# Latent heads of block 1: where 1 / z is multiplied in a two-block transformer kernel

## The chip, the core and the metric
The kernel runs on one core of one Trainium2 chip. The metric is the time of one execution in device microseconds (us): 780.84 us is the median of three runs of the kernel before, 778.87 us and 781.52 us are the lowest and the highest. A smaller time is better. Engines are called as the profile calls them: PE (matrix products), DVE, ACT and POOL (element-wise work), SP (issues the DMAs).

## The reference, cut to what matters
Two transformer blocks are computed for 256 latent tokens of width 1024, with 256 context tokens in the first block. The change lies in the first block's second group of heads, the latent heads (`B_HEADS = 8`), whose queries and keys come out of low-rank projections:

```python
def _softmax_attend(q, k, v):
    scale = (B_NOPE + B_ROPE) ** -0.5
    s = jnp.einsum('bqhd,bkhd->bhqk', q, k).astype(jnp.float32) * scale
    a = jax.nn.softmax(s, axis=-1)
    return jnp.einsum('bhqk,bkhe->bqhe', a.astype(v.dtype), v)
```

q has 256 rows and k and v 512 (context and latent tokens together), a head's q and k are 96 wide, v is 64 wide. The softmax is exp(s - max) divided by its sum z along a row. The outputs of these heads and of the four differential heads (`_diff_attend`) are joined and multiplied by `w_out`; then come a gated feed-forward layer, a norm, and the second block.

## The kernel before
Activations are kept with channels on the 128 partitions and tokens along the free axis. A weight matrix is streamed in pieces of 1 MB into `raw` buffers (three of them), and every half of a piece is split into a rounded part `hi` (ACT copies) and a rest `lo` (DVE subtracts); a linear layer issues three products for each 128x128 block (`lin`, `wout_part`).

All instructions are recorded first and put in order by a planner (`Rec.schedule`, from line 485): a list scheduler with costs of its own for every instruction (`cost`, from line 439), which starts at each step the instruction that can start earliest, and breaks ties by the order of the program. It knows that two-input instructions of DVE and those of POOL can hold each other up ("port" in `cost`). For the tags in `STRICT` (`raw`, `hi`, `lo`, `la`, `tp`, `mm`, `s`, `v5` among them) buffers are given out in the order of the program. Every engine then runs its own list in order. Since all instructions are emitted by one line (666), the profile's groups are told apart by their tiles: `s` and `v` (for `v5`) are score banks, `tp` is a pair of banks for transposes and small sums, `la` is the single bank of an attention output, `mm` holds linear layers, `c` is any tile of 256 or 512 columns, `col` one of a few columns.

The stage of the latent heads runs over four pairs (`for hp in range(4)`, line 1328). `unit(softB2, pvB2, hp)` records the softmax of both heads of a pair, and then the output of the pair before it (`flush`). `softB` does, for each of two tiles of 128 queries (`qt`): scores 128x512 into a bank, a row maximum (DVE), its scaling (DVE), the exponential with the row sum z (ACT), the reciprocal of z (DVE), and a multiplication of the 128x512 probabilities by it: on POOL for `qt` 0, on DVE for `qt` 1 (`POOL_B = (0,)`). `pvB2` transposes the probabilities of both heads with the identity into `tp` banks, four 128x128 transposes to a bank (`transposed`, line 1162), copies each bank out on ACT, multiplies by `vB` into `la`, head 0 of the pair on the output rows 0 to 63 and head 1 on rows 64 to 127, and splits the result into the `hi` and `lo` halves of a tile of `cat`.

Beside these heads run the end of the differential heads, `gemv` (line 975: rows of `ada2` in a `raw` buffer times a row vector `crow`; after `h0` the pieces 7, after `h1` 8 and 9, after `h3` 10 and 11; for all of these but 9 the product is POOL's, 128x1024, twice for each piece, and ACT sums it), and the parts of `w_out` on finished tiles of `cat` (`wout_part`: two after pair 1, two after pair 2, two after pair 3, two after the last output). Behind the stage come the other half of `w_out` (banks `s` and `v5`), the residual, and the feed-forward layer.

Of the kernel before, what the change touches and what calls it, by code (L numbers as in the profile page):

```python
# [14 lines left out]
AF = mybir.ActivationFunctionType  # L15
OP = mybir.AluOpType
# [200 lines left out]
POOL_A, POOL_B, POOL_N = (1,), (0,), (0, 1)  # L217
# [461 lines left out]
def _build(ctx, tc, nc, A, out):  # L679
# [7 lines left out]
    V, ACT, G, PE, SP = (rec.eng(e) for e in ("V", "ACT", "G", "PE", "SP"))  # L687

    def own(pool, name, tag, shape, dt):

        def make():
            t = f"{tag}s{v.root.slot}"
            return pool.tile(shape, dt, tag=t, name=name, bufs=1)
        v = rec.root(tag, shape, dt, make)
        return v

    def T(tag, shape, dt=F32):
        cnt[0] += 1
        name = f"{tag}_{cnt[0]}"
        return own(sp, name, tag, shape, dt)  # L700
# [7 lines left out]
    def PS(tag, shape):  # L708
        cnt[0] += 1
        name = f"{tag}_{cnt[0]}"  # L710
        return own(pp, name, tag, shape, F32)

    def mm(o, a, b, start, stop):
        PE.matmul(o, a, b, start=start, stop=stop)

    def mm2(o, a, b, start, stop):
        return PE.matmul(o, a, b, start=start, stop=stop, skip_group_check=True)
# [3 lines left out]
    def PSR(shape, tags):  # L721
        k = rot[tags] = rot.get(tags, -1) + 1
        return PS(tags[k % len(tags)], shape)
# [4 lines left out]
    def c1(dt=F32, n=256):  # L728
        return T("c1", [128, n], dt)

    def c2(dt=F32):
        return T("c2", [128, 512], dt)
# [24 lines left out]
    ident = cst.kid((slice(None), slice(0, 128)))  # L757
# [209 lines left out]
    def split(dst_h, dst_l, src):  # L967
        ACT.activation(dst_h, src, AF.Copy)
        V.tensor_tensor(dst_l, src, dst_h.bitcast(F32), OP.subtract)
# [192 lines left out]
    def transposed(p):  # L1162

        r = []
        for kp in range(2):
            tp = PS("tp", [128, 512])
            for z in range(2):
                kt = 2 * kp + z
                for qt in range(2):
                    o = 256 * z + 128 * qt  # L1170
                    PE.transpose(tp[:, o:o + 128], p[qt][:, 128 * kt:128 * kt + 128], ident)
            t = c2()
            ACT.activation(t, tp, AF.Copy)
            r += [t[:, 0:256], t[:, 256:512]]
        return r

    cat = []
    scA, scB = 64 ** -0.5, 96 ** -0.5
# [40 lines left out]

    def softB(h):  # L1220
        pa = []
        for qt in range(2):
            tq = slice(128 * qt, 128 * qt + 128)
            mx = T("col", [128, 4])
            s_ = PSR([128, 512], SC)
            mm(s_, qB[h][0:96, tq], kB[h][0:96], True, True)
            V.tensor_reduce(mx[:, 0:1], s_, AX.X, OP.max)
            V.tensor_scalar(mx[:, 1:2], mx[:, 0:1], -scB, None, op0=OP.mult)
            p = c2()
            ACT.activation(p, s_, AF.Exp, bias=mx[:, 1:2], scale=scB, accum_out=mx[:, 2:3])  # L1230
            V.reciprocal(mx[:, 3:4], mx[:, 2:3])
            (G if qt in POOL_B else V).tensor_scalar(p, p, mx[:, 3:4], None, op0=OP.mult)
            pa.append(p)
        return pa

    def softB2(hp):
        return softB(2 * hp), softB(2 * hp + 1)

    def pvB2(hp, pas):
        o_ = PS("la", [128, 256])  # L1240
        aT = [transposed(pa) for pa in pas]
        for kt in range(4):
            for z in range(2):
                h = 2 * hp + z
                mm2(o_[64 * z:64 * z + 64], vB[kt][:, 64 * h:64 * h + 64], aT[z][kt], kt == 0, kt == 3)
        c_ = c2(F32R)
        split(c_[:, 0:256], c_[:, 256:512], o_)
        cat.append(c_)

    pend = []  # L1250
# [77 lines left out]
    for hp in range(4):  # L1328
        unit(softB2, pvB2, hp)
        gemvs(f"h{hp}")  # L1330
        for kc in WOUT_AT.get(hp, ()):
            wout_part(kc)
# [21 lines left out]
    for m in range(8):  # L1354
        if m < 4:
            ps = woa[m // 2][:, m % 2]
        else:
# [7 lines left out]
                               op0=OP.mult, op1=OP.subtract)  # L1365
# [154 lines left out]
    for m in range(8):  # L1520
# [6 lines left out]
                               op0=OP.mult, op1=OP.subtract)  # L1527
# [270 lines left out]
    for qt in range(2):  # L1798
# [21 lines left out]
        o_ = PS("la", [128, 512])  # L1820
        gs = [slice(0, 64), slice(64, 128)]
        tp = PS("tp", [128, 128])
# [4 lines left out]
        for j in range(4):  # L1827
            p = [(c2 if qt else c1)().rearrange("p (a b) -> p a b", a=2) for _ in range(2)]
            mx, zs = T("col", [128, 8]), T("col", [128, 2, 2])
# [12 lines left out]
            for br in range(2):  # L1842
                for g in range(2):
                    ACT.activation(p[g][:, br, 0:nk], p[g][:, br, 0:nk], AF.Exp, bias=mx[:, 4 + 2 * br + g:5 + 2 * br + g],
                                   accum_out=zs[:, br, g:g + 1])
# [9 lines left out]
        for kt in range(qt + 1):  # L1855
            for br in range(2):
                n_ += 1
                ts = []
                for g in range(2):
                    tp = PS("tp", [128, 512])  # L1860
# [34 lines left out]
    for m in range(4):  # L1895
# [5 lines left out]
        s_ = c2(F32R)  # L1901
# [6 lines left out]
    for m in range(8):  # L1908
        pb = PSR([128, 256], LIN)
        lin(pb, BASE["proj"] + 8 * m, 4, lambda kc: nsa[kc][:, 0:256], lambda kc: nsa[kc][:, 256:512])  # L1910
        pa = PSR([128, 256], LIN)
        lin(pa, BASE["proj"] + 8 * m + 4, 4, lambda kc: ssm[kc][:, 0:256], lambda kc: ssm[kc][:, 256:512])
        s_ = sg[m]
# [60 lines left out]
```

## Time and profile before

| | us |
|---|---|
| median of three runs | 780.84 |
| lowest and highest run | 778.87, 781.52 |
| the profiled execution, its own time | 778.39 |
| span of the profiled execution, first to last instruction | 776.6 |
| PE busy in the span | 743.9 (96%) |
| DVE busy | 583.5 (75%) |
| ACT busy | 430.8 (55%) |
| POOL busy | 304.9 (39%) |

The span is 1.8 us shorter than that execution's own time. Busy shares are averages over stages with different limits. Matmuls are pipelined and their ends are modelled, so a PE that is shown busy need not be at its peak. The stage of the latent heads lies between about 144 us and 194 us. Groups are read by tile names, for the reason given above. "Idle before" beside an instruction is the time in which its engine had nothing to run, with what ended it.

### The profile page before, as it was taken

Reading aid. Unit: us, or ns where it says so; the run is one execution under the profiler, and the core shown is the slowest. Engines: PE = TensorE matmul, PEld = TensorE weight load, DVE = VectorE, ACT = ScalarE, POOL = GpSimd, SP = SyncE. Lnnn points to the kernel's source line nnn. Section 1 sums busy time; section 2 is a strip of 40 time slices with the busy share of each in tenths; the row PEclk is TensorE's granted clock in tenths of the full one; section 3 lists DMA queues with packets and bytes.
Section 4 is the critical chain, followed back from the end, with each engine's and each line's share of the span. In section 5 each row is a group of like instructions: output and inputs, shape, how many; then the busy total and the mean of one; then the engine's idle time right before and its main releaser. Section 6 shows DMA issues by size and latency. Waiting matters only on the chain.

```text
span 776.6 us, 15213 instructions
## 1 busy us (share of the span) xinstructions
PE 743.9 (96%) x5987; PEld 675.2 (87%) x5987; DVE 583.5 (75%) x1106; ACT 430.8 (55%) x786; POOL 304.9 (39%) x313
## 2 busy tenths in 40 slices
PE   5998999999999999999999997899999999999998
PEld 3877785557999999999999996498899999999997
DVE  6768787977999899888668898976488666654552
ACT  6435439887765365555554432578556666643441
POOL 0013154764041949998012175686250333310000
PEclk9999899999999999999999999999999999999999
DMA  8956633434597366554666621053364655556540
GB/s 332 364 212 229 217 132 114 177 108 176 204 270 273 110 257 230 181 201 167 214 227 214 214 84 55 1 170 157 110 208 173 213 172 212 180 208 199 203 176 14
DMA packets 33993, 142.88 MB, mean 184 GB/s; under 512 B 11777, under 2 KB 15233, under 8 KB 17794
## 3 DMA queue, kind: packets, MB, share of 16 engines
q1 hardware_dynamic: 33922, 141.91, 51.7%
q8 instruction: 47, 0.77, 0.4%
q14 instruction: 24, 0.20, 0.1%
HBM read 139.54 MB, written 1.05 MB: 181 GB/s over the span
## 4 chain that ended last, share of the span: by engine, by line
PE 86%; DVE 8%; ACT 3%; DMA 1%; issue 1%; POOL 0%; SPq 0%; DVEq 0%
PE mm L666 42%; PE s L666 32%; PE tp L666 6%; DVE c L666 5%; PE la L666 4%; PE v L666 3%; ACT c L666 2%; DVE lo L666 1%; DVE col L666 1%; DMA raw<-in_ada 1%; DMA k_X<-in_x 0%; DVE raw L666 0%; DVE k_adc L666 0%; ACT raw L666 0%; ACT hi L666 0%
## 5 line engine op out<-in xcount | busy, mean ns | idle before, releaser
L666 DVE TENSOR_TENSOR lo<-raw,hi 128x1024 fp32r<-128x1024 f32 x206 | 263.0, 1280 | 82.3 <-ACT hi L666 81.0
L666 ACT ACTIVATE hi<-raw 128x1024 fp32r<-128x1024 f32 x206 | 216.2, 1053 | 193.1 <-PE mm L666 94.3
L666 PE MATMUL mm<-xs,hi 128*128 128x256 f32 (+1 forms) x992 | 179.6, 282 | 0.6 <-ACT hi L666 0.4
L666 PEld LDWEIGHTS mm<-xs,hi 128*128 128x128 f32 x992 | 151.4, 188 | 3.2 <-issue 1.4
L666 PE MATMUL mm<-c,hi 128*128 128x256 f32 (+1 forms) x744 | 141.8, 289 | 4.6 <-DVE c L666 2.7
L666 PE MATMUL mm<-xs,lo 128*128 128x256 f32 (+1 forms) x496 | 138.5, 280 | 2.0 <-DVE lo L666 2.0
L666 PEld LDWEIGHTS mm<-c,hi 128*128 128x128 f32 x744 | 115.1, 190 | 14.3 <-issue 4.7
L666 PE MATMUL s<-xs,hi 128*128 128x256 f32 (+1 forms) x672 | 123.0, 283 | 0.0
L666 PE MATMUL s<-c,hi 128*128 128x256 f32 (+1 forms) x676 | 120.2, 278 | 0.0
L666 PE MATMUL mm<-c,lo 128*128 128x256 f32 (+1 forms) x372 | 106.4, 287 | 1.2 <-DVE lo L666 1.2
L666 PEld LDWEIGHTS s<-c,hi 128*128 128x128 f32 x676 | 103.2, 188 | 1.4 <-issue 0.4
L666 PEld LDWEIGHTS s<-xs,hi 128*128 128x128 f32 x672 | 102.9, 188 | 0.7 <-issue 0.4
L666 PEld LDWEIGHTS mm<-xs,lo 128*128 128x128 f32 x496 | 93.8, 189 | 2.8 <-DVE lo L666 2.2
L666 PE MATMUL s<-xs,lo 128*128 128x258 f32 (+1 forms) x336 | 94.1, 280 | 2.2 <-DVE lo L666 2.2
L666 PE MATMUL s<-c,lo 128*128 128x256 f32 x338 | 94.2, 279 | 0.0
L666 ACT ACTIVATE c<-c 128x256 fp32r<-128x256 f32 (+4 forms) x141 | 61.7, 448 | 57.4 <-DVE c L666 54.4
L666 POOL TENSOR_TENSOR raw<-raw,k_crow 128x1024 f32<-128x1024 f32 x18 | 48.0, 2668 | 111.7 <-DMA raw<-in_ada 100.2
L666 DVE TENSOR_TENSOR c<-c,c 128x256 fp32r<-128x256 f32 (+2 forms) x115 | 65.0, 577 | 20.1 <-POOL c L666 15.7
L666 POOL TENSOR_TENSOR c<-c 128x256 f32<-128x256 f32 x40 | 41.7, 1042 | 89.2 <-ACT c L666 79.0
L666 PEld LDWEIGHTS mm<-c,lo 128*128 128x128 f32 x372 | 70.7, 191 | 3.0 <-DVE lo L666 1.6
L666 PEld LDWEIGHTS s<-xs,lo 128*128 128x128 f32 x336 | 63.8, 190 | 2.9 <-DVE lo L666 2.6
L666 PEld LDWEIGHTS s<-c,lo 128*128 128x128 f32 x338 | 63.5, 188 | 0.3
(251 smaller groups left out, 1119.4 us busy)
## 6 DMA issues: line engine op xcount, KB each, us to landing
raw<-in_wseq SPq DMA_DIRECT2D x102, 1024.0 KB, 4.8
raw<-in_ada SPq DMA_DIRECT2D x20, 1024.0 KB, 4.9
tab<-in_ada SPq DMA_DIRECT2D x4, 1024.0 KB, 7.4
c<-in_w SPq DMA_DIRECT2D x8, 256.0 KB, 4.6
k_X<-in_x SPq DMA_DIRECT2D x4, 256.0 KB, 4.8
raw<-in_wseq SPq DMA_DIRECT2D x2, 512.0 KB, 8.0
tab<-in_ctx SPq DMA_DIRECT2D x4, 256.0 KB, 10.6
out<-c SPq DMA_DIRECT2D x7, 128.0 KB, 2.4
```

The costliest lines, as they stand in the source:

```text
L666: getattr(self.real[o.eng], o.fn)(*[val(x) for x in o.args], **{k: val(x) for k, x in o.kw.items()})
```

## The change
The probabilities of the latent heads are no longer multiplied by 1 / z. `softB` keeps the two row sums of a head side by side (`rz[:, 0:2]`), makes one reciprocal of both, and hands it on. In `pvB2` four products are added ahead of the output's own: for each head of the pair and each tile of queries, a column of 1 / z, repeated 64 times, is multiplied with the identity, which yields 64 rows that each hold the 128 values of 1 / z along the free axis. The four fill a 128x256 `tp` tile (`rr`), laid out as the pair's output. ACT copies it to SBUF (`rb`), DVE multiplies the output in `la` by it, and the split into halves then reads this product from SBUF, not from `la`.

```diff
     def softB(h):
         pa = []
+        rz = T("col", [128, 4])
         for qt in range(2):
             tq = slice(128 * qt, 128 * qt + 128)
-            mx = T("col", [128, 4])
+            mx = T("col", [128, 2])
...
             p = c2()
-            ACT.activation(p, s_, AF.Exp, bias=mx[:, 1:2], scale=scB, accum_out=mx[:, 2:3])
-            V.reciprocal(mx[:, 3:4], mx[:, 2:3])
-            (G if qt in POOL_B else V).tensor_scalar(p, p, mx[:, 3:4], None, op0=OP.mult)
+            ACT.activation(p, s_, AF.Exp, bias=mx[:, 1:2], scale=scB, accum_out=rz[:, qt:qt + 1])
             pa.append(p)
-        return pa
+        V.reciprocal(rz[:, 2:4], rz[:, 0:2])
+        return pa, rz
...
     def pvB2(hp, pas):
         o_ = PS("la", [128, 256])
-        aT = [transposed(pa) for pa in pas]
+        aT = [transposed(pa) for pa, _ in pas]
+
+        rr = PS("tp", [128, 256])
+        for qt in range(2):
+            for z in range(2):
+                mm2(rr[64 * z:64 * z + 64, 128 * qt:128 * qt + 128], pas[z][1][:, 2 + qt:3 + qt].to_broadcast([128, 64]), ident, True, True)
+        rb = c1()
+        ACT.activation(rb, rr, AF.Copy)
         for kt in range(4):
             for z in range(2):
                 h = 2 * hp + z
                 mm2(o_[64 * z:64 * z + 64], vB[kt][:, 64 * h:64 * h + 64], aT[z][kt], kt == 0, kt == 3)
+        V.tensor_tensor(rb, o_, rb, OP.mult)
         c_ = c2(F32R)
-        split(c_[:, 0:256], c_[:, 256:512], o_)
+        split(c_[:, 0:256], c_[:, 256:512], rb)
         cat.append(c_)
```

## Rows read from the trace of the kernel before

**Rows 1.** The page, part 1: busy time of each engine, share, instructions.

```profile
PE 743.9 (96%) x5987; PEld 675.2 (87%) x5987; DVE 583.5 (75%) x1106; ACT 430.8 (55%) x786; POOL 304.9 (39%) x313
```

**Rows 2.** Busy time by stretches of 10 us; then granted clock, DMA share, GB/s.

```profile
160.00:170.00 10.00, 8.63 (x46) 4.54 (x45) 9.21 (x20) 7.26 (x18) 4.15 (x3) 1.00 0.32 105
170.00:180.00 10.00, 9.41 (x52) 5.53 (x53) 8.29 (x18) 8.72 (x20) 8.10 (x6) 1.00 0.38 113
180.00:190.00 10.00, 9.96 (x83) 8.37 (x80) 8.89 (x10) 6.86 (x13) 4.74 (x2) 1.00 0.52 193
190.00:200.00 10.00, 10.00 (x83) 8.89 (x83) 6.47 (x15) 7.26 (x23) 0.00 (x0) 1.00 0.87 324
```

**Rows 3.** Chain of waits, 155 to 205 us: start, length, engine and tile.

```profile
163.98 2.92 DVE c L666 x2
...
167.00 0.79 ACT c L666 x2
...
173.42 1.63 DVE c L666
```

**Rows 4.** DVE in order of time: start, length, instruction, count [idle before].

```profile
162.30 0.48 DVE L666 TENSOR_SCALAR c<-c,col 128x512 f32<-128x512 f32 x1
...
164.24 2.66 DVE L666 TENSOR_SCALAR c<-c,col 128x512 f32<-128x512 f32 x1
...
182.63 2.40 DVE L666 TENSOR_SCALAR c<-c,col 128x512 f32<-128x512 f32 x1
```

**Rows 5.** POOL in order of time, a product of a `gemv`.

```profile
164.26 2.35 POOL L666 TENSOR_TENSOR raw<-raw,k_crow 128x1024 f32<-128x1024 f32 x1 [4.07 <-DMA raw<-in_ada]
```

**Rows 6.** PE in order of time: the four idle times named in the text.

```profile
151.70 1.98 PE L666 MATMUL s<-c,c 96*128 96x512 f32 x4 [0.67 <-ACT c L666]
...
163.65 0.63 PE L666 MATMUL tp<-k_cst,c 128*128 128x128 f32 x4 [0.22 <-ACT c L666]
...
167.83 1.12 PE L666 MATMUL s<-c,c 96*128 96x512 f32 x2 [1.16 <-ACT c L666]
...
179.38 1.06 PE L666 MATMUL tp<-k_cst,c 128*128 128x128 f32 x8 [0.59 <-ACT c L666]
```

**Rows 7.** DVE groups, 157 to 194 us, shapes apart: count, busy us, mean ns, idle.

```profile
L666 DVE TENSOR_SCALAR c<-c,col 128x512 f32<-128x512 f32 x8 | 11.2, 1413 | 0.0
...
L666 DVE RECIPROCAL col<-col 128x1 f32<-128x1 f32 x11 | 1.7, 157 | 1.7 <-ACT c L666 1.5
L666 DVE TENSOR_TENSOR c<-la,c 128x256 fp32r<-128x256 f32 x3 | 1.2, 415 | 0.5 <-ACT c L666 0.5
```

**Rows 8.** POOL groups, 120 to 194 us, shapes apart.

```profile
L666 POOL TENSOR_SCALAR c<-c,col 128x512 f32<-128x512 f32 x11 | 18.9, 1723 | 17.8 <-PE la L666 9.2 <-DVE col L666 6.5 <-PE mm L666 2.0
```

**Rows 9.** PE in order of time: products with 64 and with 32 output rows.

```profile
164.21 0.65 PE L666 MATMUL la<-c,tab 128*64 128x256 f32 x2
...
165.59 1.08 PE L666 MATMUL la<-c,tab 128*64 128x256 f32 x8
...
168.88 1.08 PE L666 MATMUL la<-c,tab 128*64 128x256 f32 x6
...
182.68 1.95 PE L666 MATMUL la<-c,tab 128*64 128x256 f32 x16
...
460.04 3.69 PE L666 MATMUL tp<-c,c 128*32 128x128 f32 x64
```

**Rows 10.** ACT groups, 157 to 194 us, shapes apart.

```profile
L666 ACT ACTIVATE c<-la 128x256 fp32r<-128x256 f32 x4 | 1.5, 380 | 0.5 <-PE la L666 0.5
...
L666 ACT ACTIVATE c<-c 128x256 fp32r<-128x256 f32 x1 | 0.4, 438 | 0.0
L666 ACT ACTIVATE c<-la 128x256 f32<-128x256 f32 x1 | 0.4, 410 | 0.0
```

**Rows 11.** DVE in order of time: one form, beside a POOL product and without.

```profile
145.78 2.22 DVE L666 TENSOR_TENSOR k_adc<-k_adc,k_pc 128x8 f32<-128x8 f32 x1
...
191.45 0.17 DVE L666 TENSOR_TENSOR k_adc<-k_adc,k_pc 128x8 f32<-128x8 f32 x1 [2.04 <-ACT raw L666]
```

## The prediction

> **What bounds the kernel now.** I read the page first: PE is busy for 96% of the span, so whatever a change takes from another engine is worth only the idle time of PE that it closes, and whatever it gives PE costs its full length wherever PE is full [rows 1]. Next I read the stage by stretches of 10 us [rows 2]. From 160 to 180 us PE is busy for 8.63 and 9.41 us, DVE for 9.21 and 8.29, ACT for 7.26 and 8.72: three engines close to full and none at its limit. From 180 us on PE is at 9.96 and 10.00. So the stage has two halves: up to about 180 us the engines wait for each other, and behind it PE alone decides, with `w_out` as its filler. The granted clock is 1.00 in all four, so the clock is no part of the matter.
>
> The chain of waits says who is late in the first half: a piece of 2.92 us on DVE, then ACT's exponential that stood behind it, later another 1.63 us on DVE [rows 3]. In order of time these are the very multiplications that the change removes: one of them takes 0.48 us when nothing is in its way and 2.66 us when it starts together with a POOL product on a `raw` tile [rows 4, 5]. The row maximum of the next scores stands behind it on DVE, the exponential behind that, and PE behind the exponential. What reaches PE is less than what DVE lost, since PE has other products to issue: its idle times of the stage are 0.67, 0.22, 1.16 and 0.59 us [rows 6]. This is the stock from which a gain can come.
>
> **Removed from DVE and POOL.** Eight multiplications of 128x512 leave DVE: 8 x 1.413 = 11.3 us [rows 7], of which 8 x 0.48 = 3.8 us is work [rows 4] and 7.5 us is standing still. Eight leave POOL, 8 x 1.72 = 13.8 us [rows 8]. Sixteen reciprocals become eight: 8 x 0.157 = 1.3 us less on DVE [rows 7]. None of this is a saving in itself. What it is worth is PE's idle time behind it. Of the four idle times the first (0.67, at 151.7 us) stands before the first of these multiplications on DVE, so I leave it as it is. The other three make 0.22 + 1.16 + 0.59 = 1.97 us. They are a little larger than shown, because an end is modelled: eight transposes are shown with 1.06 us and four with 0.63, so one more costs 0.11 us, while a lone one would be shown with 0.30 [rows 6]; up to 0.17 us is hidden at each gap, 0.5 us for three. Recoverable at most 2.5 us, at least nothing.
>
> The transposes also no longer wait for the scaled probabilities, and POOL reaches its `gemv` products sooner, so that `raw` buffers come free and the weights of `w_out` arrive sooner: PE's filler, which now begins at about 180 us, can move into the first half. That speaks for taking nearly all of it: I take 2.5 us.
>
> **Added to PE.** Four products for each pair, sixteen in all. PE issues a product of plain fp32 as two instructions (an output of a pair, eight products, is x16). The trace has no product with 64 output rows and 128 columns, so I bound it. From below: products with 32 output rows and the same 128 columns, two of them side by side on different rows, took 3.69 us for 64 instructions, 0.115 us for two side by side [rows 9]; a pair's eight instructions are four such, 0.46 us. The nearest row by shape is an output with 64 rows and twice the columns, 1.95 us for 16 instructions, 0.24 us for two side by side [rows 9]; half the columns give 0.12, four of them 0.49 us. From above: the two heads' products are not side by side, because the second head's 1 / z comes later; then eight times 0.115, 0.92 us. I take 0.49, the row nearest in shape, 4 x 0.49 = 2.0 us in all, with 1.8 and 3.7 us as ends. Nothing covers this: the last pairs lie in the half in which PE is full.
>
> **Added to ACT and DVE.** ACT copies `rr`, 4 x 0.41 = 1.6 us, and the copy in the split reads SBUF, 0.44 in place of 0.38 us, 0.2 us in all [rows 10]: 1.8 us. Spread over four pairs this is 0.46 us each, against 2.7 and 1.3 us of idle time of ACT in the two stretches [rows 2]; I cost it at nothing, and if ACT is what PE waits for, at the first rival. DVE gets four products of `la` with `rb`, at the price of the instruction of nearest form, 4 x 0.415 = 1.7 us [rows 7], far less than what it loses. `rr` takes a turn in the two `tp` banks, so the next pair's transposes wait for its copy; and the product on DVE waits for both PE and that copy, with the next pair's row maxima queued behind it. On the other side `la` comes free at that product; now its second reader is the subtraction behind ACT's copy. The end of the stage gets longer by one step of 0.42 us between the last output and its split; there PE is at 10.00 with `w_out` [rows 2], which hides it, and without that cover it would cost the 0.42 us. No DMA is added or moved; SP's order of loads follows the `raw` buffers.
>
> **The sum.** -2.5 + 2.0 = -0.5 us. The profiled execution would go from 778.39 to 777.9 us, and the median, which lies 2.45 us above that execution, from 780.84 to 780.3 us. Bounds of this case: all of the idle time with the cheapest products, -2.5 + 1.8 = -0.7; half of it, -1.25 + 2.0 = +0.8.
>
> **A rule against it.** The trace shows a two-input DVE instruction on 128x8 with 0.17 us in one place and 2.22 us beside a POOL product [rows 11]; it is not a multiplication by a column, yet it stood still as long. The Trainium skill (SBUF — State Buffer, Who interferes with whom) says that a DVE instruction with two SBUF inputs contends with a GpSimd instruction that reads SBUF, and that whichever is issued first blocks the other to its end; the trace agrees, by 2.05 us. By that rule the split's subtraction, which now has one input in PSUM, becomes such an instruction. This kernel would then exchange eight stalls for four, which is the second rival below.
>
> **The rivals.** *Slower: the products lie apart and ACT takes DVE's place.* If the 1 / z of the two heads come at different times, the planner issues the products of one head alone, 3.7 us in all, and PE's idle times, all of them ended by ACT [rows 6], shrink only by a third (0.8 us), because ACT, at 8.72 us of 10 already, now has 1.8 us more to do. 3.7 - 0.8 = +2.9 us, 783.7 us. It decides from the point at which the products cost over 3.1 us while less than 0.8 us comes back. For it: ACT ended every one of the four idle times. Against it: ACT itself was idle for 2.7 us in 160 to 170 us [rows 2], when DVE was late.
>
> *No change, and no relief: the port stall moves.* The four subtractions with two SBUF inputs each meet a POOL product and stand for up to 2.05 us [rows 11], 4 x 2.05 = 8.2 us against the 7.5 us that go. Nothing of PE's idle time comes back and the products remain: +2.0 us, 782.8 us. Against it: POOL has 13.8 us less to do, and the subtraction comes late in a pair.
>
> *Faster: outputs close up as well.* An output of a pair now comes in pieces, where the two heads' probabilities are ready at different times: the first pair's 16 instructions took 0.65 + 1.08 + 1.08 = 2.81 us, in one piece they take 1.95 [rows 9]. If every transpose comes early, two pairs save 0.6 us each after the modelled ends, and all four idle times close, 2.64 + 0.7 = 3.3 us: -3.3 - 1.2 + 1.8 = -2.7 us, 778.1 us. It needs PE to be full through the whole stage, for which nothing in the first half of it is an example [rows 2].
>
> **How the numbers follow.** A measurement of this kernel can tell about 0.3%, 2.3 us, from no change. Chances: the forecast 0.45 and the moved stall 0.20, both within 0.3%; faster 0.17; slower 0.18. So same is 0.65. The forecast's bounds, -0.7 and +0.8, together with the moved stall's +2.0 hold 0.65; for 0.8 the range has to reach the nearer parts of the two outer cases, at -2.7 and +2.9: 778.0 to 783.6 us.
>
> **What would show it.** Right: no 128x512 multiplication on DVE and POOL between 143 and 190 us beside that of the last differential head, no DVE gap of 2 us ahead of a row maximum, 64-row products into `tp` at 0.46 to 0.5 us for each pair, PE's three idle times behind 155 us under 0.5 us together, and the first feed-forward product within 1 us of where it was. Wrong: products apart by heads, idle times of PE before 180 us that are as long as before or longer, subtractions of over 1 us behind `la`, or a difference that arises behind the first feed-forward product, where the change touches nothing and only the planner's order could move.

## The result and the profile after

The changed kernel takes 783.35 us, the median of 18 runs (778.93 to 788.66), against 778.23 us for the kernel before in 18 runs beside it: a ratio of 1.0063, 95% interval 1.0045 to 1.008. It is slower by 0.63%, 4.9 us. The forecast was "no change".

The profiled execution of after took 788.66 us (span 786.9, mean granted clock 0.987); that of before 778.39 us at 0.995. It is the longest of its 18, so a second profile of after was taken (e1, below), and both are read. Part 1 of the page of after, to set beside [rows 1]:

```profile
PE 751.8 (96%) x6019; PEld 682.2 (87%) x6019; DVE 578.1 (73%) x1094; ACT 432.1 (55%) x790; POOL 293.0 (37%) x305
```

DVE is busy for 5.4 us less and POOL for 11.9 us less, as intended, and PE has 32 instructions more. But PE is busy for 7.9 us more, and 16 more fp32 products were to cost 2.0. That is the first sign that something else happened to PE.

To see where, I cut each trace at five PE instructions that every kernel has: the first `mm<-lo,c` product of 512 columns (143.05 us in before; PE's order is the same in all kernels up to there), the first product of 258 columns (the feed-forward layer's first half, 205.99 us), the last of these (339.13 us), the first `xs` product of 256 columns behind the layer (block 2, 399.11 us), and the first such product of the last layer (598.13 us). "Low" is the time at the lower of the two clock levels, 1.2 GHz, within the stretch. The second half of the layer took 60.0 us, and the end, from the last cut to PE's last product, 174.7 us in every profile, so they are left out.

| stretch (us) | before | after | after again (e1) |
|---|---|---|---|
| up to the stage | 143.05, low 6.8 | 141.50, low 3.4 | 146.39, low 13.7 |
| stage | 62.94 | 68.45, low 3.4 | 62.77 |
| feed-forward, first half | 133.13 | 135.38, low 3.4 | 133.24 |
| block 2, to the last layer | 199.01 | 203.05, low 10.2 | 202.45, low 6.8 |

The stretch ahead of the stage differs by chance: nothing in it was changed, and over the 18 profiles of this document it takes 139.9 to 147.7 us, the longer the more of it is at the low clock. The stage is 5.5 us longer in one profile of after and 0.2 us shorter in the other.

Stretches of 10 us of after, where [rows 2] show before (columns as there):

```profile
160.00:170.00 10.00, 10.00 (x61) 6.26 (x60) 9.70 (x18) 8.71 (x20) 6.79 (x3) 1.00 0.53 201
170.00:180.00 10.00, 8.22 (x62) 5.91 (x61) 4.69 (x9) 7.72 (x21) 3.85 (x2) 1.00 0.55 192
180.00:190.00 10.00, 10.00 (x64) 6.47 (x63) 7.21 (x17) 8.59 (x22) 0.00 (x0) 1.00 0.64 219
190.00:200.00 10.00, 10.00 (x89) 9.24 (x89) 2.79 (x6) 4.34 (x8) 0.00 (x0) 1.00 0.36 117
```

PE in order of time in the stage of after, its three idle times that are not in e1's profile at such a length (idle before in brackets, with what ended it):

```profile
149.85 0.39 PE L666 MATMUL mm<-c,lo 128*128 128x256 f32 x1 [1.62 <-DVE lo L666]
...
152.31 1.92 PE L666 MATMUL s<-c,c 96*128 96x512 f32 x2 [1.04 <-ACT c L666]
...
173.64 0.66 PE L666 MATMUL tp<-k_cst,c 128*128 128x128 f32 x4 [1.78 <-ACT c L666]
```

What DVE did ahead of them, in the same profile:

```profile
146.35 3.44 DVE L666 TENSOR_TENSOR lo<-raw,hi 128x1024 fp32r<-128x1024 f32 x1
...
165.79 2.55 DVE L666 TENSOR_TENSOR c<-c,c 128x256 fp32r<-128x256 f32 x1
...
168.86 2.77 DVE L666 TENSOR_TENSOR lo<-raw,hi 128x1024 fp32r<-128x1024 f32 x1
...
172.85 1.28 DVE L666 TENSOR_TENSOR c<-c,c 128x256 fp32r<-128x256 f32 x1
```

The subtraction at 165.79 us is the split of the last differential head, which the kernel before has too (0.42 us there). The one at 172.85 us is the first of the four new ones, the split of the first pair of latent heads.

The same `lo` in e1, and POOL beside it, first in after and then in e1:

```profile
151.25 1.21 DVE L666 TENSOR_TENSOR lo<-raw,hi 128x1024 fp32r<-128x1024 f32 x1
```

```profile
144.03 4.68 POOL L666 TENSOR_TENSOR raw<-raw,k_crow 128x1024 f32<-128x1024 f32 x2
```

```profile
148.93 5.77 POOL L666 TENSOR_TENSOR raw<-raw,k_crow 128x1024 f32<-128x1024 f32 x2
```

In after POOL runs the two products of `gemv` 8 back to back (4.68 us for both) and DVE's `lo` stands for 3.44 us; in e1 `lo` comes between them, takes 1.21 us, and POOL needs 5.77. Same program, and a different engine goes first. The Trainium skill (SBUF — State Buffer, Who interferes with whom) says that issue order decides which of the two blocks. These four rows agree that one engine stands while the other works; which was issued first they do not show. In after the granted clock then fell at 152.5 us for 3.4 us. This bad start of the stage appears in one of the eleven profiles that have the new stage (two of these with the gate of e4).

### The profile page after: what moved, and what is told of

It reads as the page before. It is cut to its first block, busy times and chain, and to the rows that moved or that the text cites. A ratio compares the mean times of both kernels' runs of the same rounds, so it can differ in the third digit from the quotient of the medians.

```text
span 786.9 us, 15228 instructions
## 1 busy us (share of the span) xinstructions
PE 751.8 (96%) x6019; PEld 682.2 (87%) x6019; DVE 578.1 (73%) x1094; ACT 432.1 (55%) x790; POOL 293.0 (37%) x305
## 4 chain that ended last, share of the span: by engine, by line
PE 85%; DVE 9%; issue 2%; ACT 2%; DMA 2%; POOL 0%; SPq 0%; DVEq 0%; ACTq 0%; POOLq 0%
PE mm L666 41%; PE s L666 31%; PE tp L666 6%; DVE c L666 4%; PE la L666 4%; PE v L666 3%; DVE lo L666 2%; ACT c L666 1%; DMA raw<-in_wseq 1%; DVE col L666 1%; DVE raw L666 1%; DMA raw<-in_ada 1%; ACT hi L666 0%; DVE k_adc L666 0%; SPq L666 0%
## 5 line engine op out<-in xcount | busy, mean ns | idle before, releaser
L666 ACT ACTIVATE c<-c 128x256 fp32r<-128x256 f32 (+5 forms) x145 | 63.4, 447 | 60.8 <-DVE c L666 57.9
L666 DVE TENSOR_TENSOR c<-c,c 128x256 fp32r<-128x256 f32 (+2 forms) x119 | 69.3, 594 | 20.4 <-POOL c L666 15.7
```

The source lines that it names most:

```text
L666: getattr(self.real[o.eng], o.fn)(*[val(x) for x in o.args], **{k: val(x) for k, x in o.kw.items()})
```

## Experiments

All ran beside the kernel before. "Ratio" is to before, with the 95% interval; "clock" is the mean granted clock of the timed runs (0.993 to 0.994 for before). The median of before was 779.02 us beside e1 to e4, 778.13 us beside e5 to e8, 778.01 us beside e9 to e12 and 779.16 us beside e13 to e16, so runs of different groups are compared by their ratios. "Stage" and "layer" (the feed-forward layer's first half, and the low-clock time in it) are cut from each kernel's profile as above; for e3 (*) the cut falls at another place, see there.

| run | median us | ratio | clock | stage | layer |
|---|---|---|---|---|---|
| after | 783.35 | 1.0063 (1.0045–1.008) | 0.990 | 68.45 | 135.38, low 3.4 |
| e1 after again | 784.18 | 1.0043 (1.0021–1.0065) | 0.989 | 62.77 | 133.24 |
| e2 no multiplication | 778.25 | 0.9987 (0.9966–1.0007) | 0.992 | 61.12 | 133.16 |
| e3 only what is added | 781.83 | 1.0043 (1.0019–1.0068) | 0.993 | 62.53* | 137.85* |
| e4 `gemv` 8 gated | 786.15 | 1.0070 (1.0045–1.0096) | 0.989 | 63.01 | 137.19, low 3.4 |
| e5 new stage, old tail | 778.49 | 1.0002 (0.9971–1.0033) | 0.994 | 62.97 | 133.13 |
| e6 old stage, new tail | 781.28 | 1.0042 (1.0013–1.0072) | 0.990 | 63.20 | 133.81 |
| e7 before, another plan | 781.64 | 1.0052 (1.0021–1.0083) | 0.992 | 62.93 | 135.65, low 3.4 |
| e8 after, another plan | 780.65 | 1.0028 (1.0004–1.0052) | 0.990 | 62.73 | 133.60, low 3.4 |
| e9 new stage, new block 2 | 779.14 | 1.0007 (0.9976–1.0038) | 0.995 | 62.91 | 133.16 |
| e10 new stage, new layer | 781.14 | 1.0020 (0.9992–1.0049) | 0.992 | 62.71 | 135.36, low 3.4 |
| e11 e3 with old tail | 782.40 | 1.0034 (1.0013–1.0056) | 0.992 | 65.04 | 133.21 |
| e12 e5 with the gate | 778.78 | 1.0001 (0.9973–1.003) | 0.993 | 62.89 | 133.16 |
| e13 after, one `lo` ahead | 779.58 | 1.0009 (0.9985–1.0034) | 0.992 | 62.85 | 131.85 |
| e14 e10, one `lo` ahead | 777.91 | 0.9985 (0.9958–1.0012) | 0.992 | 62.74 | 131.84 |
| e15 before, two `lo` ahead | 778.89 | 0.9995 (0.9969–1.002) | 0.992 | 62.95 | 134.35, low 3.4 |
| e16 e5, two `lo` ahead | 776.65 | 0.9992 (0.9961–1.0024) | 0.994 | 62.96 | 132.44 |

### First group: the parts of the change

e1 is the kernel after once more, with no edit.

> The changed kernel once more, for a second profile and a second interval. All theories: 4 to 6 us longer than the kernel before. Theory A (POOL, freed of its multiplications, issues the two products of gemv 8 back to back, and the weight rest lo stands behind them on DVE): the profile shows again a lo of over 3 us at about 146 us, and PE idle for over 1.5 us right behind it. Theory B (the added products on PE and what hangs on them): that place can differ, the 64-row products cost 2.0 to 2.6 us in all. Theory C (the granted clock falls by chance in other places): a clear spread of the time from profile to profile that follows the mean clock.

The loss repeats (1.0043), with a stage of 62.77 us. So the stage of the first profile is not where it comes from as a rule.

e2 leaves out the division by z in the latent heads: the multiplications are planned and not issued.

```diff
-        for i in order:
+        for i in [i for i in order if i not in self.skip]:
...
-            (G if qt in POOL_B else V).tensor_scalar(p, p, mx[:, 3:4], None, op0=OP.mult)
+            rec.skip.add((G if qt in POOL_B else V).tensor_scalar(p, p, mx[:, 3:4], None, op0=OP.mult).i)
```

> The kernel before with the order of its plan, but the sixteen multiplications of the probabilities are not issued, and nothing takes their place: the latent heads are left without 1 / z. It does the removal alone. Theory A: POOL runs both products of gemv 8 back to back here too, the lo stands for over 3 us, and the gain is small or none: -1 to +2.5 us. Theory B: PE gets its idle time back and pays nothing, -2.0 to -2.5 us.

The stage falls by 1.82 us. That is the relief without its price. The whole kernel is not told from before (0.9987, 0.9966 to 1.0007), so its time does not decide between the two theories.

e3 keeps the multiplications and adds what the change adds, with ones in place of 1 / z.

```diff
+        rr = PS("tp", [128, 256])
+        for qt in range(2):
+            for z in range(2):
+                mm2(rr[64 * z:64 * z + 64, 128 * qt:128 * qt + 128], ones[:, 0:64], ident, True, True)
+        rb = c1()
+        ACT.activation(rb, rr, AF.Copy)
...
+        V.tensor_tensor(rb, o_, rb, OP.mult)
         c_ = c2(F32R)
-        split(c_[:, 0:256], c_[:, 256:512], o_)
+        split(c_[:, 0:256], c_[:, 256:512], rb)
```

> The kernel before with its multiplications, and on top of it the sixteen short products (of a column of ones with the identity), the copy to SBUF, the product of the output with it (by 1.0), and the split from SBUF. It does the addition alone. Theory A: +2.0 to +2.6 us, the length of the products on PE. Theory B: +4.5 to +5.5 us, nearly the whole difference.

It is 0.43% slower, 3.4 us. By the cuts all of it lies in the layer (137.85 us against 133.13) and none in the stage, but in e3 the layer's first product runs ahead of 22 of the 72 instructions on bank `s` that end `w_out`:

```profile
207.41 0.40 PE L666 MATMUL mm<-xs,hi 128*128 128x258 f32 x2
...
210.05 0.28 PE L666 MATMUL s<-c,lo 128*128 128x256 f32 x1
```

At three instructions in 0.34 us these are 2.5 us. Counted to the stage, as in the other kernels, they make it 65.0 us and the layer 135.4 us (an estimate): +2.1 us in the stage, and +2.2 us in the layer, of which nothing was edited. This second part is where I began to doubt the place. e4 holds POOL's second `gemv` 8 product back, the theory made from the profile of after:

```diff
+    pooled = {}
...
-                G.tensor_tensor(wz, wz, crow, OP.mult)
+                pooled[i, z] = G.tensor_tensor(wz, wz, crow, OP.mult)
...
-    cat = []
+    cat, exps, held = [], [], {}
...
-            ACT.activation(p, s_, AF.Exp, bias=mx[:, 1:2], scale=scB, accum_out=rz[:, qt:qt + 1])
+            exps.append(ACT.activation(p, s_, AF.Exp, bias=mx[:, 1:2], scale=scB, accum_out=rz[:, qt:qt + 1]))
...
+    for k, n in {(8, 1): 2}.items():
+        pooled[k].deps.add(exps[n].i)
     rec.issue()
```

> The changed kernel, in which the second POOL product of gemv 8 waits for the third exponential of the latent heads, so that the two are no longer back to back. Theory A: the lo at about 146 us takes under 1.5 us, PE's idle time behind it shrinks by about 1.8 us, and the kernel takes 2 to 3.5 us less than the changed one, so +1.5 to +3 us against the one before. Theory B: no difference to the changed kernel, +4 to +6 us.

It did not help (1.0070). `lo` took 1.21 us and the stage is as long as in before, but the layer has grown by 4 us. As the cause of the loss, that theory falls; since the gate also changed the order behind the stage, e12 below is the clean test of it.

### Second group: the stage or what is behind it

The planner orders the whole program. A changed duration in the stage gives other orders behind it: PE's order of after differs from before's from the stage until 2066 instructions before the end. These runs hold the planner to a given order for all that is recorded behind the latent heads ("the tail": the second half of `w_out`, the feed-forward layer and block 2), engine by engine; `TAIL` is that order, read from the plan of one kernel or the other. Held to its own tail, each kernel keeps its own order on every engine.

```diff
                 for pr, i in sorted(h)[:60]:
+                    if i >= self.tail and TAIL[e][turn[e]] != i - self.tail:
+                        continue
                     o = ops[i]
...
             h.remove((pr, i))
+            turn[e] += i >= self.tail
...
+    rec.tail = len(rec.ops)
     sums = {}
```

e5 is after with before's tail:

> The kernel after, but the planner is held to the order of the kernel before for everything that is recorded behind the stage (second half of w_out, feed-forward, block 2), engine by engine; the stage itself is planned as in after. Theory S (the stage costs it: products on PE and the port): 782.5 to 784.5 us, ratio 1.0045 to 1.008, as after. Theory T (what is behind the stage costs it: another order there, with more waits of PE in the feed-forward layer and more time at the low clock): 777.7 to 779.5 us, ratio 0.9995 to 1.0015, since the stage of the second profile of after is 0.2 us shorter than that of before. Half and half: 780 to 781.5.

e6 is before with after's tail:

> The kernel before, but held behind the stage to the order in which the kernel after runs what is recorded there; the multiplications on DVE and POOL remain, no product is added. Theory S: the time of before, 777.5 to 779 us, ratio 0.999 to 1.001. Theory T: 781.5 to 784 us, ratio 1.004 to 1.007, with a mean granted clock near 0.989 as in after. Half and half: 779.5 to 781.

Both came out on the side of theory T: 1.0002 with the new stage and the old tail, its interval ending (1.0033) below the start of that of after; 1.0042 with the old stage and the new tail, its interval clear of 1, and its median just under the range given. The loss moves with the order behind the stage, not with the change. e7 and e8 change only one planned duration behind the stage, in before and in after.

```diff
     rstd_of(rsf[:, 0:256], st, D)
+    rec.ops[-1].dur += 0.2
```

> The kernel before with one duration in the planner, that of an ACT instruction behind the stage, larger by 0.2 us; no instruction differs, the orders are the same up to the end of the stage and other ones from there to the middle of block 2. How far does another order alone move the time? Theory S: within 0.1% of before. Theory T: by 1 to 4 us to either side, with another mean granted clock.

> The kernel after with the same duration in the planner larger by 0.4 us, which gives it another order behind the stage. Theory S: as after, 782.5 to 784.5 us. Theory T: by 1 to 4 us away from after, likelier down than up, if after's order there was an unlucky one.

(e8 adds 0.4.) The kernel before, with not one instruction changed, becomes 0.5% slower by another order. After comes out at 1.0028; that interval overlaps the one of after, so a gain is not shown.

The stage of e5 shows what the change does by itself. Stretches of 10 us, to set beside [rows 2]:

```profile
160.00:170.00 10.00, 10.00 (x62) 5.99 (x61) 9.18 (x17) 8.69 (x22) 8.34 (x4) 1.00 0.50 170
170.00:180.00 10.00, 10.00 (x66) 6.79 (x66) 3.90 (x9) 7.71 (x16) 2.35 (x1) 1.00 0.59 217
180.00:190.00 10.00, 10.00 (x77) 7.59 (x76) 5.89 (x15) 8.54 (x25) 0.00 (x0) 1.00 0.46 175
190.00:200.00 10.00, 10.00 (x89) 9.24 (x88) 5.01 (x14) 5.34 (x14) 0.00 (x0) 1.00 0.30 107
```

PE in e5, its only idle time of over 0.2 us between 144 and 206 us, and the first of the four sets of new products with the instruction behind it:

```profile
151.64 1.13 PE L670 MATMUL s<-c,c 96*128 96x512 f32 x2 [0.71 <-ACT c L670]
...
164.63 0.66 PE L670 MATMUL tp<-k_cst,col 128*64 128x128 f32 x8
165.11 1.25 PE L670 MATMUL la<-c,tab 128*64 128x256 f32 x10
```

PE is full from 160 us on: 40.0 us of 40 where before had 38.0. The three idle times behind 155 us are gone, 2.0 us, and a set of eight product instructions takes 0.48 us to the next start, 1.9 us for four. The stage takes 62.97 us against 62.94.

### Third group: which half of the tail, and the price of the products

e9 and e10 take one kernel's order up to the last product of the layer's first half, and the other's behind it; only `TAIL` differs from e5.

> The stage of after, then before's order up to the last product of the feed-forward layer's first half, then after's order for what is left (its second half and block 2). Same instructions as in e5, in another order behind that point only. If the loss lies in block 2: 781 to 784 us, ratio 1.003 to 1.007, with two drops of the clock between 475 and 500 us. If it lies in the feed-forward layer: 778 to 779.5 us, ratio 0.9995 to 1.0015. If it is in both by halves: 780 to 781.

> The counterpart: the stage of after, after's order up to the last product of the feed-forward layer's first half, before's order for what is left. If the loss lies in block 2: 778 to 779.5 us. If it lies in the feed-forward layer: 781 to 784 us, with a drop of the clock between 270 and 280 us, and idle times of PE of over 2 us ahead of it. By halves: 780 to 781.

1.0007 and 1.0020: by their medians the loss would lie in the layer, but with intervals of 0.3% to each side the shares are not settled. The profile of e10 has a drop of the clock in the layer, that of e9 none. Nor has e9's any in block 2, which takes 199.90 us in after's order there; the two profiles with before's order and no drop in block 2 show 199.01 (before) and 198.93 us (e16). So the order of block 2 alone costs 0.9 us, as far as three profiles tell. e11 is e3 with before's tail:

> The kernel of e3 (multiplications kept, the products, the copies and the extra product on DVE added, with ones in place of 1 / z) with before's order behind the stage. It prices what the change adds, with nothing removed and nothing else moved. The forecast's step says +2.0 us on PE with ends of +1.8 and +3.7: 780.1 us, 779.9 to 781.8, ratio 1.0025. If the price of e3 (+3.6 us) was mostly its order behind the stage: below 780.5. If ACT's and DVE's parts cost on top: over 781.8.

The stage takes 65.04 us, +2.10, at the forecast's price; the three idle times of before are still there, 1.6 us of 2.0:

```profile
163.28 0.63 PE L670 MATMUL tp<-k_cst,c 128*128 128x128 f32 x4 [0.22 <-ACT c L670]
...
167.39 1.13 PE L670 MATMUL s<-c,c 96*128 96x512 f32 x2 [0.87 <-ACT c L670]
...
179.49 0.63 PE L670 MATMUL tp<-k_cst,c 128*128 128x128 f32 x4 [0.52 <-ACT c L670]
```

The median is 4.4 us above that of before, over the 781.8 us at which the expectation put a price on ACT and DVE too; the ratio says +2.7 us (+1.0 to +4.4), so the stage's 2.1 us alone are possible. With the estimate for e3, 2.1 us as well, the price stands in two profiles. The profile of e11 has 13.7 us at the low clock in block 2, where before's has none, with the same order there. e12 adds the gate of e4 to e5:

> The kernel of e5 with the gate of e4 (the second product of gemv 8 on POOL waits for the third exponential of the latent heads). If the long wait of DVE's lo behind POOL's two products (3.44 us in the profile of after, at 146 us) costs a share of the runs 5 us, as the profile of after would have it, the highest runs go and the median falls by 0.5 to 1.5 us against e5, to 777 to 778 us. If that profile was one chance run: as e5, 778.5 us.

No difference to e5 (1.0001, 1.0002): the race for the port at the start of the stage is no steady cost.

### Fourth group: one instruction

The layer has PE's idle times at places that the order sets. Before, PE in order of time, all idle times of over 0.2 us between 206 and 339 us (e2, e5, e9, e11, e12 have the same three within 0.02 us):

```profile
262.38 0.51 PE L666 MATMUL mm<-xs,hi 128*128 128x258 f32 x2 [0.38 <-ACT hi L666]
...
263.93 0.39 PE L666 MATMUL s<-xs,lo 128*128 128x258 f32 x1 [1.03 <-DVE lo L666]
...
283.58 0.39 PE L666 MATMUL s<-xs,lo 128*128 128x258 f32 x1 [1.16 <-DVE lo L666]
```

After (e1, e6 and e10 have the middle one with 2.08 or 2.09; the last is 0.18 us in e1, 0.71 in e6 and 0.75 in e10):

```profile
269.35 0.39 PE L666 MATMUL mm<-xs,lo 128*128 128x258 f32 x1 [0.50 <-DVE lo L666]
...
274.34 0.39 PE L666 MATMUL s<-xs,lo 128*128 128x258 f32 x1 [2.09 <-DVE lo L666]
...
308.14 0.39 PE L666 MATMUL s<-xs,lo 128*128 128x258 f32 x1 [0.76 <-DVE lo L666]
```

DVE in after, ahead of the 2.09 us:

```profile
269.98 0.50 DVE L666 SCALAR_TENSOR_TENSOR c<-c,c 128x256 f32<-128x256 f32 x1
270.97 0.95 DVE L666 TENSOR_TENSOR c<-c,c 128x256 fp32r<-128x256 f32 x1 [0.49 <-ACT c L666]
272.29 0.43 DVE L666 TENSOR_TENSOR c<-mm,k_rsf 128x258 f32<-128x258 f32 x1 [0.36 <-PE mm L666]
272.75 0.21 DVE L666 TENSOR_SCALAR c<-c 128x1 f32<-128x1 f32 x1
272.88 2.96 DVE L666 TENSOR_TENSOR lo<-raw,hi 128x1024 fp32r<-128x1024 f32 x2
```

The `lo` that PE needs next is queued behind a subtraction that waits for ACT and behind the read of a product that PE has only just finished. So PE runs dry: it must finish, DVE must read, then make `lo`, and only then has PE work. In this profile the granted clock falls right behind it, in e1 it does not. Stretches of 4 us of after, then of e1:

```profile
270.00:274.00 4.00, 2.25 (x19) 2.04 (x17) 3.12 (x5) 0.93 (x2) 3.77 (x5) 1.00 0.71 262
274.00:278.00 4.00, 3.66 (x21) 3.67 (x22) 4.00 (x5) 2.00 (x2) 3.92 (x4) 0.67 0.21 61
278.00:282.00 4.00, 4.00 (x32) 4.00 (x32) 2.86 (x5) 1.68 (x3) 3.92 (x4) 0.90 0.63 221
```

```profile
270.00:274.00 4.00, 1.93 (x16) 1.72 (x15) 3.41 (x5) 1.32 (x3) 3.84 (x5) 1.00 0.59 246
274.00:278.00 4.00, 4.00 (x36) 4.00 (x35) 4.00 (x4) 1.70 (x3) 3.92 (x3) 1.00 0.48 139
```

e13 moves that one `lo` three places ahead; every other engine's order is the same. In `TAIL` of after's own order (917 is that `lo`; in before's order it stands ahead of all the others shown):

```diff
-         ... 881, 882, 884, 886, 913, 914, 917, 953, ...
+         ... 881, 882, 884, 917, 886, 913, 914, 953, ...
```

> The kernel after, its own order on every engine, but for one DVE subtraction (lo<-raw,hi, at 272.88 us of the profile of after) which goes three places ahead, before the c<-c,c at 270.97 us and the read of PE's product at 272.29 us. No other instruction moves. Theory W (PE's wait of 2.25 us for it, and the drop of the clock behind it, cost the feed-forward layer's share): the wait falls below 0.5 us, no drop between 255 and 300 us, the layer's first half takes 131 to 131.5 us, and the median falls by 2 to 4 us, to 779.5 to 781.5 us. Rival O (the order as a whole, many small waits): the layer is shorter by 1 us at most, the median 782.5 to 784.

DVE in e13, and PE's idle times:

```profile
270.58 0.50 DVE L670 SCALAR_TENSOR_TENSOR c<-c,c 128x256 f32<-128x256 f32 x1
271.01 2.32 DVE L670 TENSOR_TENSOR lo<-raw,hi 128x1024 fp32r<-128x1024 f32 x1
273.24 0.83 DVE L670 TENSOR_TENSOR c<-c,c 128x256 fp32r<-128x256 f32 x1
274.00 0.41 DVE L670 TENSOR_TENSOR c<-mm,k_rsf 128x258 f32<-128x258 f32 x1
```

```profile
269.94 0.39 PE L670 MATMUL mm<-xs,lo 128*128 128x258 f32 x1 [0.50 <-DVE lo L670]
...
273.38 0.39 PE L670 MATMUL s<-xs,lo 128*128 128x258 f32 x1 [0.52 <-DVE lo L670]
```

2.09 us became 0.52, no drop follows in the layer, and the layer takes 131.85 us against 133.24 (e1, no drop) and 135.38 (after, drop). The wait and the layer miss theory W's figures by a little (below 0.5, 131 to 131.5 us), the median meets them. The ratio is 1.0009 (0.9985 to 1.0034). After and e1, the same kernel, give 1.0055 together, weighted by their intervals (1.0042 to 1.0069): a gain of 3.6 us, 1.4 to 5.8. That is theory W, although the profiled execution of e13 is the longest of its 12 (784.70 us, with 13.7 us at the low clock ahead of the stage and 6.8 us in block 2). e14 does the same in e10:

> The kernel of e10 (stage and feed-forward order of after, block 2 in the order of before) with the same one DVE instruction three places ahead. Theory W: 777 to 779 us, against 781.14 us of e10. Rival O: 780 to 781.5 us.

777.91 us, as theory W had it: 0.9985 after 1.0020 for e10, though these two intervals overlap. e15 and e16 move two `lo` of before's order ahead (856 over 825, 852 and 853; 1043 over 1039), in before and behind the stage of after.

```diff
-         ... 821, 823, 825, 852, 853, 856, ... 1010, 1039, 1043, ...
+         ... 821, 823, 856, 825, 852, 853, ... 1010, 1043, 1039, ...
```

> The kernel before, its own orders, but for two DVE subtractions (lo<-raw,hi at 262.38 and 282.31 us of its profile), moved ahead of the instructions that wait for ACT and PE (three places and one place). Theory W: PE's idle times of 1.03 and 1.1 us ahead of 263.93 and 283.58 us go, the layer's first half takes 130.5 to 131.3 us against 133.1, and the median falls by 1.8 to 2.6 us, to 775.5 to 776.5 us, ratio 0.9965 to 0.998. Rival O: within 0.5 us of before.

> The kernel of e5 (the stage of after, before's order behind it) with the two DVE subtractions of e15 moved ahead. Theory W: as e15, 775.5 to 776.8 us, since the stages of both kernels take the same time. Rival O: as e5, 778.5 us.

These did not do what I expected of them. DVE and PE in e15:

```profile
259.46 2.07 DVE L670 TENSOR_TENSOR lo<-raw,hi 128x1024 fp32r<-128x1024 f32 x1
261.44 1.26 DVE L670 TENSOR_TENSOR c<-c,c 128x256 fp32r<-128x256 f32 x1
262.63 0.41 DVE L670 TENSOR_TENSOR c<-mm,k_rsf 128x258 f32<-128x258 f32 x1
```

```profile
263.19 0.77 PE L670 MATMUL mm<-xs,hi 128*128 128x258 f32 x2 [2.34 <-DVE c L670]
```

The first `lo` took 2.07 us beside a POOL product, and now the read that frees PE's bank stands behind it: two idle times of 0.38 and 1.03 us became one of 2.34. The second move worked (1.16 us became 0.35 in e15, nothing in e16). The median of e16 lies in the range of theory W, but three of its twelve runs took over 783 us, and its ratio, 0.9992, is not told from 1. By accident the two make a pair for the clock. Stretch behind the idle time, in e15 and in e16, which has the same 2.34 us:

```profile
262.00:266.00 4.00, 2.81 (x13) 2.84 (x14) 3.96 (x5) 0.51 (x1) 3.77 (x4) 0.64 0.04 4
```

```profile
262.00:266.00 4.00, 3.21 (x27) 3.24 (x28) 3.96 (x5) 0.51 (x1) 3.77 (x4) 1.00 0.12 12
```

With the drop the layer takes 134.35 us, without it 132.44; 0.35 us of the difference is the second place. One drop costs about 1.6 us here. The order of after has a second such pair, after and e6, whose idle times are nearly the same:

```profile
263.02 0.39 PE L670 MATMUL mm<-xs,lo 128*128 128x258 f32 x1 [0.56 <-DVE lo L670]
...
268.00 0.39 PE L670 MATMUL s<-xs,lo 128*128 128x258 f32 x1 [2.08 <-DVE lo L670]
...
300.17 0.39 PE L670 MATMUL s<-xs,lo 128*128 128x258 f32 x1 [0.71 <-DVE lo L670]
```

There it is 135.38 - 133.81 = 1.6 us again; e1 is shorter still, 133.24 us, because it lacks the last idle time. Over the 18 profiles, a drop in the layer came with an idle time of 2.08 us or more in six of nine, and in none of the nine whose longest was 1.86 us or less. This is a count for the layer and no threshold: in block 2 no idle time is longer than 1.95 us, and 15 of the 18 profiles have a drop there, whatever the order.

None of these is shown to beat the kernel before: e14, the best ratio, is 0.9985 with 1 inside its interval. It does beat the kernel after, as its interval ends at 1.0012 and that of after begins at 1.0045.

## Why the prediction was wrong

**The direction of the call.** "Same" was forecast as likeliest, and against the 780.84 us of before the range of 778.0 to 783.6 us is a ratio of 0.9964 to 1.0035; it is 1.0063. That 783.35 us lies within the range in microseconds is luck: the median of three runs on which it was built, 780.84 us, lies 2.6 us above that of the 18 runs of before beside after. What the prediction said of the stage holds, and the sum was made for the stage only.

**Removed from DVE and POOL: right, a little too large.** 2.5 us were taken from PE's idle time, 1.97 shown and 0.5 hidden under modelled ends. e5 against e11, which has the multiplications, differs by 65.04 - 62.97 = 2.07 us; e2 against before gives 1.82. So 1.8 to 2.1 us came back.

**Added to PE: right.** 2.0 us forecast, 2.10 us measured (e11 against before), with the two heads' products side by side in every pair. The *slower* rival's condition, products apart by heads, did not occur. That of the *faster* one, PE full, did from 160 us on, but its -2.7 us did not come: closing up the outputs gave nothing that the stage shows.

**ACT and DVE at nothing: right within the stage.** PE was at 10.00 in each stretch of e5.

**The sum of the stage.** -0.5 us forecast, +0.03 measured in e5, and -0.2 in e1.

**The moved stall: one of four, and it cost nothing there.** The rival stood at +2.0 us, with the four new subtractions each held up by a POOL product. Only the first one was: 1.28 us in after, 1.11 in e1, 1.22 in e5; the other three took 0.42 or 0.43 us in each. In e5 and e1 PE had other products meanwhile. The Trainium skill's rule on two SBUF inputs (SBUF — State Buffer, Who interferes with whom) stood beside this rival; the first subtraction, which ran beside POOL's products, agrees. Its sign, a subtraction of over 1 us, so came once in each of the three profiles, without its price. The longer stalls of after, 2.55 and 2.77 us, belong to a subtraction and a `lo` that the kernel before has too. As a steady cost of the stage this rival is out; such stalls took part in the one profile with the bad start.

**The step that failed: what lies behind the stage was valued at nothing.** "What would show it" named "a difference that arises behind the first feed-forward product, where the change touches nothing and only the planner's order could move" as a sign of being wrong, and no term, rival or width of the range stood for it. That is what happened: e5 and e6 show it by exchange (1.0002 and 1.0042), and e13 shows that the place of one DVE instruction in the new order is worth 1.4 to 5.8 us. From the profiles about 1.6 us of this is PE's wait, and 1.6 us is the drop behind it in those runs that have one. Against before the wait is no loss by itself, because before's order has waits of its own, 2.57 us in all: without a drop the layer took 133.24 and 133.81 us in after's order, 133.13 to 133.21 in before's. With a drop it took 135.4 us, in two of four profiles of after's order and in none of six of before's, too few to prove the share. With block 2's 0.9 us this makes about 2.2 us on the mean of the four profiles, of the 4.3 us (3.3 to 5.4) by which after and e1 together are slower. So the order is shown as the cause; the drops as its main way are argued, and the rest is open. e7 prices the term that was missing: before's own program moved by 0.5% under another order. With 0.5% more to the slow side the range would have reached a ratio of 1.0085 and held the result.

**The clock.** "The clock is no part of the matter" was read from four stretches of the stage. It holds there and not behind it: the mean over the timed runs is 0.993 for before and 0.990 for after. How much of the loss goes with it can be estimated from the single runs. The 34 runs of before beside e1 are 5.2 us longer for each 0.01 of the mean clock that they lack, the 35 beside e6 6.1 us. By that about 2 us go with the lower clock of e1 (0.9890 against 0.9927) and as much with that of e6 (0.9904 against 0.9937), of 4.4 and 3.6 us between the means; 2.5 and 1.6 us are there at an equal clock.

**What stays open.** How the rest divides between the layer and block 2: e9 and e10 do not settle it. The low clock in block 2 came with after's order there (10.2 us in after, 6.8 in e1, e6 and e13, none in e9) and with before's (6.8 us in e5, 13.7 in e11, none in before), so the order alone does not decide it. How often the start of the stage costs 5 us, as in the first profile, was not counted; e12 against e5 shows no steady cost.

## What to carry to other kernels

Where one planner orders the whole program, an edit is two changes: the work, and a new order behind it. Price the second by a neutral disturbance (a planned duration changed by 0.2 us moved this kernel by 0.5%), or hold the order behind the edit fixed, before you judge the edit. When PE waits for DVE, look at what the needed instruction is queued behind: one that waits for PE's own last product makes PE run dry, and moving it ahead was worth more than the edit itself. Check what it is moved past as well: in e15 the same move made a longer wait.

## What was not expected of the hardware

- An idle time of PE of 2.1 us in the middle of dense products was followed by a drop from 2.4 to 1.2 GHz in some executions and not in others with the same order there (after and e10 yes, e1 and e6 no). The drop of 3.4 us cost the layer about 1.6 us in two pairs of profiles.
- At the end of a POOL product for which DVE stands still, either DVE's instruction or POOL's next product may go first, in the same program: `lo` took 1.21 us in e1 and 3.44 us in after.
- Most idle times of PE in a fixed order repeat within 0.02 us from kernel to kernel (0.38, 1.03 and 1.16 us in six profiles with before's order, 2.08 to 2.09 us in four with after's). These belong to the order, not to chance. Not all do: the third one of after's order was 0.71 to 0.76 us in three profiles and 0.18 us in e1.
